# Fused decoder step: first tiles from unnormalised features, and a scan whose decays come from running sums read back from DRAM

## The chip, the cores and the metric

The kernel runs on one core of a Trainium2 chip. The metric is the device time of one execution in microseconds; lower is better. Before the change it is 1802.67 us, the median of three runs (1802.15 to 1803.92). One further execution was recorded by the hardware profiler.

The engines are TensorE (PE, matrix products into PSUM), VectorE (DVE), ScalarE (ACT), GpSimd (POOL) and SyncE (SP). Here SP issues the loads of weights, POOL most other transfers, and ACT a few at the start.

## What is computed

One layer of a hybrid decoder with 2048 features, on 288 tokens: 256 of one prompt and 32 samples (8 branches of 4 tokens, each with its own prior state). Cut to what matters here:

```python
n = rmsnorm(h, g_mix)
proj = n @ w_in                      # z | x, B, C | dt | u | v
xbc = silu(causal_dwconv(xbc, conv0, conv_w, conv_b))
dt = softplus(dt_raw + dt_bias);  A = -exp(a_log)
# scan, chunks of 128 tokens, 4 groups of 8 heads
acum = cumsum(dt * A)
decay = exp(where(tril, acum[l] - acum[s], -inf))
y_diag = einsum(C, B, decay, x * dt)
states = einsum(B, exp(acum[-1] - acum), x * dt)
h_next = h_prev * exp(acum[-1]) + states
y_off  = einsum(C, h_prev, exp(acum))
y = y_diag + y_off + d_skip * x
y_ssd = rmsnorm(y * silu(z))
y_cm = gelu(u) * (tril(W_s) @ rmsnorm(gelu(v)) + b_s)
h = h + concat(y_ssd, y_cm) @ w_out
# then a SwiGLU feed-forward, a gated input embedding and a final norm
```

The outputs are the features of all tokens, the new scan and convolution states, and the sample rows of v.

## The kernel before

Features lie on the 128 partitions, tokens along the free axis. A weight matrix is cut into output tiles of 128 features; each needs 16 blocks of 128x128 weights (more in the feed-forward). float32 accuracy comes from two-part numbers: a tensor is split into `hi` and `lo`, and `mm3` makes three matmuls for each block (L179 hi by hi, L180 activation lo by weight hi, L181 activation hi by weight lo). So a tile of 16 blocks is 48 matmuls of 128x128 by 288. Weights come in halves of 128x1024 (512 KB) by SP's queue into four buffers `raw` (`load`); `split_w` makes `whi` on ACT (L172) and `wlo` on DVE (L173), three buffers of each. Tiles accumulate in three PSUM banks `acc`; the small products share five banks, `big`.

The order of instructions on each engine is set by a scheduler that runs a model of the program; the text of the kernel gives the dependencies and a priority (the splits of weights are put ahead). What each engine then does is a fixed list.

**The start.** Eight slices `xin` of the input are loaded, squared on ACT (L239) and summed over the features by 48 float32 matmuls with one output column each (`sum_tokens`, L102). A chain of small DVE operations makes the norm factor, two steps on PE spread it over the partitions (L118, L120), and DVE multiplies xin by it (L249). Then each slice is split (L150 on ACT, L151 on DVE) and the matmuls of tiles 0, 1 and 2 run slice by slice, with the projection to dt among them (`pdt`, L257). `dt_work` is the softplus, `decay_work` and `decay_sample` (L313) the decays that don't depend on x.

**The scan.** There are four groups of six tiles: B, C and four of x. `conv_tile` copies a tile from PSUM into `cbuf`, applies the convolution (L338 on DVE) and the silu. Then `ssd_group`, cut by `yield` into steps that are run between weight tiles, works on a chunk: ACT writes rows R, a masked triangle times dt·A (L366); PE multiplies them by a triangle (`seg`, L371 and L372), and Exp gives the decays M. PE also transposes x (L384), forms C·B, the chunk's product M·xdt (L398), the state S, C·S of the prior state (L473), which is scaled on DVE and added by an identity matmul (L401). Samples take a segment matmul of their own (L481) and eight new states a group, each one matmul over 128 rows (`new_states`, L417).

**After the scan** come the gate, the v tiles, 16 output tiles whose result is added to h (L707), and the spatial mix. Its weights `wsr` and biases `bsr` (1 MB each) are loaded when the scan's memory is given back (`mlp_pools`, `spatial_weights`), and `wsr` is multiplied by a triangle (L576).

Of the kernel before, what the change touches and what calls it, by code (L numbers as in the profile page):

```python
# [40 lines left out]
def hybrid_step(ctx: ExitStack, tc: tile.TileContext, xT, wa, wd, wple, pT, vec, cst, wdt, dtal,  # L41
# [161 lines left out]
    rmask = csts[:, C_RM:C_RM + 8]  # L203
    TsR, UsR = csts[0:32, C_TS:C_TS + P], csts[0:32, C_US:C_US + P]
    Ts, Us = TsR[:, 0:32], UsR[:, 0:32]
# [31 lines left out]
    for q in range(8):
        sq = s0.tile([P, 2, NT], F32, tag="sq", name="sq", bufs=4)
        nc.scalar.activation(sq, xin[q], AF.Square)  # L239
        for j in range(2):  # L240
            sum_tokens(pss, sq[:, j], first=q + j == 0, last=q + j == 8)
    halves = {at: split_w(raw, 8) for at, raw in first.items()}
    nc.vector.tensor_mul(gw, wdts, bc_in(vecs[:, V_MIX:V_MIX + 16], 32))
# [4 lines left out]
    for q in range(8):
        nc.vector.tensor_mul(xin[q], xin[q], bc_mid(rs0, 2))  # L249
# [17 lines left out]
    Etm = small([P, 2, 32], "Etm")
    dec1 = small([P, 32], "dec1")
    decS = small([P, 8, 32], "decS")
    def dt_work():  # L270
        df = s0.tile([P, 384], F32, name="dtf")
        nc.scalar.copy(df[:, 0:NT], pdt[:, 0:NT])
        nc.vector.tensor_copy(r3(df[:, NT:384], 32), bc_mid(df[:, 256:288], 3))
        pd = big("pd")
# [20 lines left out]
        nc.vector.tensor_copy(dtAh, dtA)  # L295
        nc.vector.tensor_sub(dtAl, dtA, f32(dtAh))
        nc.scalar.copy(Ur, U)

    def decay_work():
        ps = big("pdec")  # L300
        nc.tensor.matmul(ps[:, 0:64], lhsT=U, rhs=dtA[:, 0:2], start=True, stop=True)
        nc.tensor.matmul(ps[:, 64:96], lhsT=UsR, rhs=dtA[0:32, 2], start=True, stop=True)
        nc.tensor.matmul(ps[:, 96:128], lhsT=T1, rhs=dtA[:, 1], start=True, stop=True)
        nc.tensor.matmul(ps[:, 128:160], lhsT=TsR, rhs=dtA[0:32, 2], start=True, stop=True)
        nc.tensor.matmul(ps[:, 160:192], lhsT=ones, rhs=dtA[:, 1], start=True, stop=True)
        nc.scalar.activation(dec.rearrange("p a b -> p (a b)"), ps[:, 0:96], AF.Exp)
        nc.scalar.activation(Etm.rearrange("p a b -> p (a b)"), ps[:, 96:160], AF.Exp)
        nc.scalar.activation(dec1, ps[:, 160:192], AF.Exp)

    def decay_sample():  # L310
        ps = big("pdec")
        for b in range(8):
            nc.tensor.matmul(ps[:, 192 + 32 * b:224 + 32 * b], lhsT=rmask[0:32, b:b + 1].to_broadcast([32, P]),  # L313
                             rhs=dtA[0:32, 2], start=True, stop=True)
        nc.scalar.activation(decS.rearrange("p a b -> p (a b)"), ps[:, 192:448], AF.Exp)
# [611 lines left out]
```

## Time and profile before

| | before |
|---|---|
| median of three runs | 1802.67 us |
| profiled execution | 1801.47 us |
| its span (first to last instruction) | 1799.3 us |
| mean granted clock of TensorE | 0.983 |
| moved by DMA | 297.63 MB, mean 165 GB/s |
| time of ACT on L172, DVE on L173 (weights) | 533.7 us, 623.3 us |

In a row of the trace the left name after the operation is the output and those behind the arrow the inputs; then come the shape and the count. Square brackets give idle time before, and what ended it. A group's row gives busy time and mean nanoseconds. Matmuls overlap, so the distance between two starts says more than a duration. The clock is a share of full speed.

### The profile page before, as it was taken

To read this page: it belongs to the slowest core of one execution; us is meant where nothing else is said; L and a number is where in the kernel's file an instruction comes from. 1 tells how busy PE (TensorE), PEld (TensorE's weight loads), DVE (VectorE), ACT (ScalarE), POOL (GpSimd) and SP (SyncE) were. 2 spreads that over 40 slices of the span, in tenths; PEclk is the share of its full clock that TensorE was granted. 3 is DMA by queue.
4 is the path that set the end of the run, shared out by engine and by line. 5 is a ranking of instruction groups with operands and counts; after the bars stand their busy time and mean duration, and the time that the engine had idled before them with its cause. 6 is when DMAs were issued, how large, how long until landed. Compare 5 with 4: busy or idle time off the path is not lost.

```text
span 1799.3 us, 31672 instructions
## 1 busy us (share of the span) xinstructions
PE 1765.1 (98%) x13084; PEld 1731.5 (96%) x13084; DVE 1062.1 (59%) x1655; ACT 826.9 (46%) x1432; POOL 31.2 (2%) x79
## 2 busy tenths in 40 slices
PE   8999999998999999999999999999999999999996
PEld 7989988978999999999999999999999999999996
DVE  3768687776445686555555554444555555554665
ACT  3585758463345544444333333333333333444452
POOL 0001010101000000000000000000000000000000
PEclk6999999999999999999999999999999999999998
DMA  4536464627555544554555545555555455555452
GB/s 161 180 132 230 133 216 143 223 88 267 165 164 165 165 135 162 165 165 158 167 164 166 165 165 159 166 163 171 167 164 168 163 168 167 161 167 169 164 166 89
DMA packets 83600, 297.63 MB, mean 165 GB/s; under 512 B 9488, under 2 KB 9616, under 8 KB 83200
## 3 DMA queue, kind: packets, MB, share of 16 engines
q1 hardware_dynamic: 75600, 268.85, 46.3%
q0 software_dynamic: 6128, 23.34, 3.6%
q10 hardware_dynamic: 1728, 3.43, 0.5%
q8 instruction: 102, 1.67, 0.4%
q14 instruction: 42, 0.34, 0.1%
HBM read 283.19 MB, written 12.39 MB: 164 GB/s over the span
## 4 chain that ended last, share of the span: by engine, by line
PE 75%; DVE 0%; ACT 0%; DVEq 0%; issue 0%
PE acc L179 25%; PE acc L181 24%; PE acc L180 24%; PE pb L597 0%; PE pb L181 0%; PE pb L179 0%; PE pb L180 0%; PE pb L589 0%; DVE h L829 0%; PE pb L102 0%; PE pb L118 0%; DVE wlo L173 0%; DVE h L707 0%; PE pb L120 0%; DVEq L916 0%
## 5 line engine op out<-in xcount | busy, mean ns | idle before, releaser
L179 PE MATMUL acc<-hi,whi 128*128 128x288 f32 x4000 | 1187.5, 297 | 7.7 <-DVE h L707 4.4
L180 PE MATMUL acc<-lo,whi 128*128 128x288 f32 x4000 | 1184.9, 296 | 0.0
L181 PE MATMUL acc<-hi,wlo 128*128 128x288 f32 x4000 | 1181.0, 295 | 1.2 <-DVE wlo L173 1.2
L172 ACT CAST whi<-raw 128x1024 fp32r<-128x1024 f32 (+1 forms) x516 | 533.7, 1035 | 827.8 <-PE acc L180 664.8
L173 DVE TENSOR_TENSOR wlo<-raw,whi 128x1024 fp32r<-128x1024 f32 (+1 forms) x516 | 623.3, 1208 | 486.2 <-ACT whi L172 479.5
L179 PEld LDWEIGHTS acc<-hi,whi 128*128 128x128 f32 x4000 | 753.1, 188 | 11.7 <-issue 7.3
L181 PEld LDWEIGHTS acc<-hi,wlo 128*128 128x128 f32 x4000 | 755.0, 189 | 3.7 <-DVE wlo L173 1.8
L180 PEld LDWEIGHTS acc<-lo,whi 128*128 128x128 f32 x4000 | 753.8, 188 | 1.5 <-issue 0.6
L783 DVE SCALAR_TENSOR_TENSOR Up<-acc,rs 128x288 f32<-128x288 f32 x44 | 20.1, 457 | 41.9 <-PE acc L181 41.9
L778 DVE TENSOR_TENSOR G<-acc,rs 128x288 f32<-128x288 f32 x44 | 20.1, 457 | 41.6 <-PE acc L181 41.6
L338 DVE SCALAR_TENSOR_TENSOR cva<-cbuf,cwh,cva 128x312 f32<-128x312 f32 x72 | 38.5, 538 | 1.3 <-ACT cva L336 0.4
L551 ACT ACTIVATE gt<-gt 128x288 f32<-128x288 f32 x32 | 14.2, 443 | 40.5 <-DVE gt L550 40.5
L389 ACT ACTIVATE xw<-xdt,dec 128x64 f32<-128x64 f32 x96 | 24.4, 338 | 5.9 <-DVE xdt L386 5.9
L102 PEld LDWEIGHTS pss<-ones,sq 128*128 128x128 f32 x96 | 20.6, 333 | 3.9 <-ACT sq L239 3.9
L102 PE MATMUL pss<-ones,sq 128*128 128x1 f32 x96 | 20.6, 352 | 3.7 <-ACT sq L239 3.7
L418 DVE TENSOR_TENSOR h<-h,pb 128x512 f32<-128x512 f32 x32 | 20.9, 680 | 1.1 <-PE pb L417 1.1
L366 ACT ACTIVATE Rh<-cst,dtAh 128x128 fp32r<-128x128 f32 x64 | 20.6, 397 | 1.5 <-PE pb L371 1.5
L784 DVE TENSOR_TENSOR Up<-Up,G 128x288 f32<-128x288 f32 x44 | 20.2, 458 | 1.5
L366 ACT ACTIVATE Rl<-cst,dtAl 128x128 fp32r<-128x128 f32 x64 | 20.8, 399 | 0.0
L424 DVE TENSOR_TENSOR h<-h,decS 128x512 f32<-128x512 f32 x32 | 20.1, 683 | 0.0
L780 DVE SCALAR_TENSOR_TENSOR G<-Gt,G 128x288 f32<-128x288 f32 x44 | 19.9, 453 | 0.1
L779 ACT ACTIVATE Gt<-G 128x288 f32<-128x288 f32 x44 | 19.4, 441 | 1.2 <-DVE G L778 1.2
(270 smaller groups left out, 927.0 us busy)
## 6 DMA issues: line engine op xcount, KB each, us to landing
raw<-in_wa_dram SPq DMA_DIRECT2D x416, 512.0 KB, 3.6
raw<-in_wd_dram SPq DMA_DIRECT2D x64, 512.0 KB, 3.5
raw<-in_wd_dram SPq DMA_DIRECT2D x32, 384.0 KB, 3.1
h<-in_h0T_dram POOLq DMA_DIRECT2D x16, 512.0 KB, 6.6
out_dram<-h POOLq DMA_DIRECT2D x16, 512.0 KB, 5.9
h<-in_xT_dram POOLq DMA_DIRECT2D x4, 576.0 KB, 7.1
raw<-in_wple_dram SPq DMA_DIRECT2D x4, 512.0 KB, 3.6
xin<-in_xT_dram ACTq DMA_DIRECT2D x4, 288.0 KB, 6.0
```

Of the source, the lines that this page charges most:

```text
L102: nc.tensor.matmul(ps[:, c:c + 1], lhsT=acc[:, t:t + P], rhs=ones[:, 0:1], start=first and c == 0, stop=last and c == 2)
L172: nc.scalar.copy(a, r)
L173: nc.vector.tensor_sub(b, r, f32(a))
L179: nc.tensor.matmul(ps, lhsT=wh, rhs=hi, start=first, stop=False)
L180: nc.tensor.matmul(ps, lhsT=wh, rhs=lo, start=False, stop=False)
L181: nc.tensor.matmul(ps, lhsT=wl, rhs=hi, start=False, stop=last)
L338: nc.vector.scalar_tensor_tensor(ao, cb[:, j:j + NCO], wt[j], ao, op0=ALU.mult, op1=ALU.add)
L366: nc.scalar.activation(cols(r, i), T1, AF.Identity, scale=f32(d[:, c, k + i:k + i + 1]))
L389: nc.scalar.activation(xw[:, 64 * h:64 * h + 64], xd[:, 64 * h:64 * h + 64], AF.Identity, scale=dec[:, c, 8 * g + h:8 * g + h + 1])
L418: nc.vector.tensor_add(h0[q][:, i], h0[q][:, i], ps)
L424: nc.vector.tensor_mul(r3(hh, 64), r3(hh, 64), bc_in(decS[:, 2 * q + i, hs], 64))
L784: nc.vector.tensor_mul(u, u, G)
```

## The change

**Start.** Tiles 0 to 5 take splits of xin times gain without the norm factor (`x_act`); the factor is multiplied in afterwards, where a tile is copied out of PSUM (now on DVE) and in `dt_work`. The loads of xin and of quarter weights alternate on SP's queue, vec and the first four xin go by ACT's, and wdt, cst, dtal and scv by POOL's. Squares are added up on DVE and summed by one set of matmuls over tokens. The normalised splits `n_act` for the later tiles are made after that.

```diff
+def first_w(m, j):
+    nc.sync.dma_start(raws[m, j // 2][:, 512 * (j % 2):512 * (j % 2) + 512],
+                      wa[m, :, 4 * j:4 * j + 4].rearrange("p k m -> p (k m)"))
+nc.scalar.dma_start(vecs, vec)
 for q in range(8):
-    (nc.scalar if q % 2 else nc.sync).dma_start(xin[q], xT[:, 2 * q:2 * q + 2])
+    (nc.scalar if q < 4 else nc.sync).dma_start(xin[q], xT[:, 2 * q:2 * q + 2])
+    if q % 2 == 0:
+        for m in range(3):
+            first_w(m, q // 2)
-        for j in range(2):
-            sum_tokens(pss, sq[:, j], first=q + j == 0, last=q + j == 8)
+            x_act.append(split(xk, gain=vcol(V_MIX, k)))
+            for m in range(3):
+                if k % 4 == 0:
+                    quarter(m, k // 4)
+                mm3(ps01[m], halves[m, k // 8], k % 8, x_act[k], k == 0, k == KD - 1)
...
+    nc.scalar.activation(sq, xin[q], AF.Square)
+    if q:
+        nc.vector.tensor_add(sqa, sqa, sq)
+nc.vector.tensor_add(sqa[:, 0], sqa[:, 0], sqa[:, 1])
+rs0 = bcast_tokens(rstd_compact(sqa[:, 0], 2048.0, EPS, "rm"))
 for q in range(8):
     nc.vector.tensor_mul(xin[q], xin[q], bc_mid(rs0, 2))
     for k in (2 * q, 2 * q + 1):
+        n_act.append(split(xin[q][:, k % 2], gain=vcol(V_MIX, k), tags=LONG))
...
-    nc.scalar.copy(df[:, 0:NT], pdt[:, 0:NT])
+    nc.vector.tensor_mul(df[:, 0:NT], pdt[:, 0:NT], rs0)
...
-    nc.scalar.copy(cb[:, 3:259], ps[:, 0:256])
+    if rs is None:
+        nc.scalar.copy(cb[:, 3:259], ps[:, 0:256])
+    else:
+        nc.vector.tensor_mul(cb[:, 3:259], ps[:, 0:256], rs[:, 0:256])
...
-    ps = ps01[at] if at < 3 else mtile(wa[at], n_act)
+    ps = ps01[at] if at < 3 else mtile(wa[at], n_act if g else x_act)
```

**Scan.** The running sums of dt·A are made once by PE, written to DRAM (`cdram`) and read back for each group onto all 128 partitions (`cq`, 8 heads by 288 tokens, 1.18 MB, on SP's queue). A decay is then Exp of −Relu(cum − cq), on ACT, and needs no x, so it is written ahead of the group's other steps. The prior state enters `y_chunk(1)` as products of S with C·exp(cum). The sample rows are packed so that a branch pair has 32 rows, and the eight new states are matmuls over 32 rows, four side by side. The small decays are one matmul set less.

```diff
-def make_R(c, hb):
...
-        nc.scalar.activation(cols(r, i), T1, AF.Identity, scale=f32(d[:, c, k + i:k + i + 1]))
-    nc.tensor.matmul(ps, lhsT=Ur, rhs=R[0], start=True, stop=False)
-    nc.tensor.matmul(ps, lhsT=Ur, rhs=R[1], start=False, stop=True)
-    nc.scalar.activation(M, ps, AF.Exp)
+            nc.scalar.activation(cols(M, i), cq[:, h, c * P:(c + 1) * P], AF.Relu, scale=-1.0,
+                                 bias=cum[:, c, 8 * g + h:8 * g + h + 1])
+        nc.scalar.activation(M, M, AF.Exp, scale=-1.0)
...
+nc.scalar.copy(crow, pc[0:32, 0:NT])
+nc.gpsimd.dma_start(cdram, crow)
...
+nc.sync.dma_start(cq, cdram[hs].unsqueeze(0).to_broadcast([P, 8, NT]))
...
-nc.tensor.matmul(ps, lhsT=cols(Cf, 1), rhs=S, start=True, stop=True)
-yoE = scaled(ps, 0)
+nc.scalar.activation(CE, CE, AF.Exp)
+nc.vector.tensor_mul(CE, CE, bc_mid(cols(Cf, 1), 8))
+nc.vector.tensor_sub(Msm, Msm, bc_in(cum[:, 2, hs], 32))
...
-            nc.tensor.matmul(cols(py, j), lhsT=cols(yoE, j), rhs=ident, start=False, stop=True)
+                l, r = (xd, cols(M[h // 4], h % 4)) if w == 0 else (off[0], off[1][:, h])
...
-nc.tensor.matmul(ps[0:32, 0:256], lhsT=Us, rhs=Rs.rearrange("p a b -> p (a b)"), start=True, stop=True)
...
-    nc.tensor.matmul(ps, lhsT=bm, rhs=xst, start=True, stop=True)
+    for q in range(4):
+        r = slice(32 * q, 32 * q + 32)
+        nc.tensor.matmul(pss[q], lhsT=bm[r], rhs=xst[r], start=True, stop=True, tile_position=(32 * q, 0))
```

**Elsewhere.** The pool of the convolution's buffers is its own, opened at the start. The product of wsr with the triangle stands in `spatial` and no longer in `spatial_weights`:

```diff
 def spatial_weights(mp):
-    nc.vector.tensor_mul(w, w, bc_mid(T1, KD))
 def spatial(nv, mp, bss, wss, w, b):
+    nc.vector.tensor_mul(w, w, bc_mid(T1, KD))
```

**The order on the engines.** First PE at the start of the program (`ps` and `acc` are the banks of the first three tiles, `pss` the sums of squares, `pb` the spread factor, `pdt` the dt projection). Before:

```order
L224 MATMUL warm<-ones 128x128 x14
L102 MATMUL pss<-ones,sq 128x1 x48
L118 MATMUL pb<-cst,rmy 128x128 x2
L120 MATMUL pb<-cst,rmy 128x32
L179 MATMUL ps_224<-hi,whi 128x288
L179 MATMUL ps_225<-hi,whi 128x288
L179 MATMUL acc<-hi,whi 128x288
L257 MATMUL pdt<-xin_82,gw 32x288 x2
```

And now, where L186 to L188 are the three lines of `mm3`, and L284 is the dt projection:

```order
L236 MATMUL warm<-ones 128x128 x14
L186 MATMUL ps_142<-hi,whi 128x288
L187 MATMUL ps_142<-lo,whi 128x288
L186 MATMUL ps_143<-hi,whi 128x288
L187 MATMUL ps_143<-lo,whi 128x288
L284 MATMUL pdt<-xin_85,gw 32x288 x2
L188 MATMUL ps_142<-hi,wlo 128x288
L188 MATMUL ps_143<-hi,wlo 128x288
```

The weight matmuls stand right behind the warm-up, with nothing for the norm ahead of them.

Next DVE, from the normalised activations on: before, the last activation lo's and then dt_work between the weight lo's.

```order
L151 SCALAR_TENSOR_TENSOR lo<-xin_89,vec,hi 128x288 x2
L273 COPY dtf<-dtf 128x96
L173 TENSOR_TENSOR wlo<-raw,whi 128x1024
L279 TENSOR_TENSOR dtwx<-pd,dtal 128x32 x3
L173 TENSOR_TENSOR wlo<-raw,whi 128x1024
L280 SCALAR_TENSOR_TENSOR dtwt<-dtwx 128x96
L173 TENSOR_TENSOR wlo<-raw,whi 128x1024
```

Now, from the second last pair of activation lo's; in front of this stand the eight products of xin (L296), the dt product (L314), three conv buffers (L382 and L383, one pair a tile) and the first twelve lo's with one weight lo:

```order
L158 SCALAR_TENSOR_TENSOR lo<-xin_91,vec,hi 128x288 x2
L158 SCALAR_TENSOR_TENSOR lo<-xin_92,vec,hi 128x288 x2
L180 TENSOR_TENSOR wlo<-raw,whi 128x1024 x2
L389 SCALAR_TENSOR_TENSOR cva<-cbuf,cwh,cva 128x312 x2
L322 TENSOR_TENSOR dtwx<-pd,dtal 128x32 x3
L389 SCALAR_TENSOR_TENSOR cva<-cbuf,cwh,cva 128x312 x2
L323 SCALAR_TENSOR_TENSOR dtwt<-dtwx 128x96
L180 TENSOR_TENSOR wlo<-raw,whi 128x1024
L389 SCALAR_TENSOR_TENSOR cva<-cbuf,cwh,cva 128x312 x2
L333 TENSOR_SCALAR dtwx<-dtwx 128x96
L325 TENSOR_SCALAR dtww<-dtwt 128x96
L382 TENSOR_TENSOR cbuf<-acc,rs 128x256
```

The convolution (`cva`) and the copies out of the banks now stand between the weight lo's, and the bank of the fourth tile is read only at the last row.

Last DVE at the first output tiles (`cvo` are the gated features, `rs` their norm factor). Before:

```order
L173 TENSOR_TENSOR wlo<-raw,whi 128x1024
L542 TENSOR_TENSOR cvo<-cvo,rs 128x288 x4
L151 SCALAR_TENSOR_TENSOR lo<-cvo,vec,hi 128x288 x4
L576 TENSOR_TENSOR wsr<-wsr,cst 128x2048
L707 TENSOR_TENSOR h<-h,acc 128x288 x3
L173 TENSOR_TENSOR wlo<-raw,whi 128x1024 x4
```

And now:

```order
L180 TENSOR_TENSOR wlo<-raw,whi 128x1024
L593 TENSOR_TENSOR cvo<-cvo,rs 128x288 x4
L158 SCALAR_TENSOR_TENSOR lo<-cvo,vec,hi 128x288 x4
L759 TENSOR_TENSOR h<-h,acc 128x288 x3
L633 TENSOR_TENSOR wsr<-wsr,cst 128x2048
L180 TENSOR_TENSOR wlo<-raw,whi 128x1024 x4
```

The product of wsr has gone from ahead of three additions to h to behind them; the weight lo's stand behind it in both.

More of the change, by code (lines that the diff above doesn't have):

```diff
@@ L202, in hybrid_step @@
     I4 = csts[:, C_I4:C_I4 + 32]
[L203 to L205 removed]
+    rmask, first8 = csts[:, C_RB:C_RB + 2], csts[:, C_R0:C_R0 + 8]
+    sgB, loB, sgX, loX = (csts[:, C_SG + i:C_SG + i + 1] for i in range(4))
+    TP, UP, TE = (csts[:, c:c + P] for c in (C_TP, C_UP, C_TE))
+    Ts = TE[:, 0:32]
     bmask = csts[:, C_BM:C_BM + 256]
@@ L294, in dt_work @@
         nc.vector.scalar_tensor_tensor(dtA, dt, -1.0, bc_mid(ea, 3), op0=ALU.mult, op1=ALU.mult)
-        nc.vector.tensor_copy(dtAh, dtA)
-        nc.vector.tensor_sub(dtAl, dtA, f32(dtAh))
-        nc.scalar.copy(Ur, U)
     def decay_work():
+        pc = big("pcum")
+        for c in range(2):
+            nc.tensor.matmul(pc[0:32, c * P:(c + 1) * P], lhsT=dtA[:, c], rhs=T1, start=True, stop=True)
+        nc.tensor.matmul(pc[0:32, 256:288], lhsT=dtA[:, 2], rhs=Ts, start=True, stop=True)
+        nc.scalar.copy(crow, pc[0:32, 0:NT])
@@ L300, in decay_work @@
+        nc.gpsimd.dma_start(cdram, crow)
         ps = big("pdec")
         nc.tensor.matmul(ps[:, 0:64], lhsT=U, rhs=dtA[:, 0:2], start=True, stop=True)
[L302 to L305, printed above, removed]
+        nc.tensor.matmul(ps[:, 64:96], lhsT=UP, rhs=dtA[:, 2], start=True, stop=True)
@@ L306, in decay_work @@
+        nc.tensor.matmul(ps[:, 96:160], lhsT=T1, rhs=dtA[:, 0:2], start=True, stop=True)
+        nc.tensor.matmul(ps[:, 160:192], lhsT=TP, rhs=dtA[:, 2], start=True, stop=True)
+        nc.tensor.matmul(ps[:, 192:224], lhsT=TE, rhs=dtA[:, 2], start=True, stop=True)
+        nc.tensor.matmul(ps[:, 224:256], lhsT=ones, rhs=dtA[:, 1], start=True, stop=True)
         nc.scalar.activation(dec.rearrange("p a b -> p (a b)"), ps[:, 0:96], AF.Exp)
-        nc.scalar.activation(Etm.rearrange("p a b -> p (a b)"), ps[:, 96:160], AF.Exp)
@@ L308, in decay_work @@
-        nc.scalar.activation(dec1, ps[:, 160:192], AF.Exp)
+        nc.scalar.copy(cum.rearrange("p a b -> p (a b)"), ps[:, 96:192])
+        nc.scalar.activation(EtmS, ps[:, 192:224], AF.Exp)
+        nc.scalar.activation(dec1, ps[:, 224:256], AF.Exp)
     def decay_sample():
+        nc.vector.tensor_mul(decS, bc_mid(dtA[:, 2], 8), bc_in(first8, 32))
         ps = big("pdec")
-        for b in range(8):
-            nc.tensor.matmul(ps[:, 192 + 32 * b:224 + 32 * b], lhsT=rmask[0:32, b:b + 1].to_broadcast([32, P]),
-                             rhs=dtA[0:32, 2], start=True, stop=True)
@@ L315, in decay_sample @@
-        nc.scalar.activation(decS.rearrange("p a b -> p (a b)"), ps[:, 192:448], AF.Exp)
+        nc.tensor.matmul(ps[:, 0:256], lhsT=ones, rhs=decS.rearrange("p a b -> p (a b)"), start=True, stop=True)
+        nc.scalar.activation(decS.rearrange("p a b -> p (a b)"), ps[:, 0:256], AF.Exp)
     sd_box = {}
@@ L323, in samples, with conv_tile @@
         return ap[:, 259:NCV].rearrange("p (b t) -> p b t", t=7)[:, :, 0:4]
-    def conv_tile(i, ps):
-        sd = sd_box["pool"]
-        cb, a, t = (sd.tile([P, NCV], F32, tag=n, name=n, bufs=b) for n, b in (("cbuf", 3), ("cva", 2), ("cvt", 2)))
+    def conv_tile(i, ps, rs=None):
+        cb, a, t = (cvp.tile([P, NCV], F32, tag=n, name=n, bufs=b) for n, b in (("cbuf", 3), ("cva", 2), ("cvt", 2)))
         nc.gpsimd.memset(cb[:, 0:3], 0.0)
@@ L432, in ssd_group @@
         brep = rep4(sd, Bf[:, 256:288])
-        R0 = [make_R(0, hb) for hb in range(2)]
+        M0 = decay(0)
         yield
@@ L514, in ssd_group @@
         for q in range(4):
-            new_states(q)
-            if q % 2:
-                yield
+            decay_h0(q)
+        yield
+        for i in range(2):
+            new_states(i)
+            yield
     ycat = [None] * 32
@@ L680, in hybrid_step @@
             at += 1
-            conv_tile(i, ps)
+            conv_tile(i, ps, None if g else rs0)
             advance(1)
```

214 lines of the change are left out of this document (118 added, 96 removed).

## The prediction

> **What bounds the kernel now.** I read the page's busy shares first, then a window over a stretch of the middle, then windows over each place where TensorE (PE) is not dense.
>
> ```profile
> PE 1765.1 (98%) x13084; PEld 1731.5 (96%) x13084; DVE 1062.1 (59%) x1655; ACT 826.9 (46%) x1432; POOL 31.2 (2%) x79
> ```
>
> ```profile
> 1000.00:1400.00 400.00, 400.00 (x3010) 400.00 (x3009) 204.55 (x248) 148.16 (x171) 0.00 (x0) 1.00 0.52 165
> ```
>
> PE is busy nearly always. The second row's columns are length, then busy time and count of PE, PE's loads, DVE (VectorE), ACT, POOL, then clock, DMA share and GB/s. In the middle, 3010 matmuls take 400 us: 0.133 us each, at full clock, with DVE half idle. The 12,000 matmuls of the weight tiles (three for each 128x128 block) are untouched by the change; at that pace they need 1595 us. What can be won is everything else: the start, stalls, and PE's small matmuls.
>
> ```profile
> 8.00:10.00 2.00, 0.00 (x0) 0.00 (x0) 0.00 (x0) 0.00 (x0) 0.00 (x0) 1.00 1.06 399
> 10.00:36.00 26.00, 22.13 (x102) 21.91 (x102) 7.04 (x18) 8.25 (x13) 0.00 (x0) 0.51 0.47 164
> 36.00:38.00 2.00, 1.12 (x7) 0.84 (x11) 2.00 (x4) 1.71 (x4) 0.00 (x0) 0.50 0.00 0
> 42.00:44.00 2.00, 2.00 (x18) 2.00 (x17) 2.00 (x6) 1.50 (x4) 0.00 (x0) 1.00 0.00 0
> 365.00:375.00 10.00, 5.54 (x27) 4.90 (x26) 5.20 (x11) 9.97 (x33) 0.00 (x0) 0.69 0.30 104
> 430.00:440.00 10.00, 5.12 (x22) 4.56 (x21) 6.79 (x7) 2.79 (x3) 0.00 (x0) 0.68 0.47 168
> 0.00:86.00 86.00, 28.78 (x96) 18.67 (x96) 0.80 0.49 170
> ```
>
> The last row counts the third matmul of each block (L181) alone: 96, six tiles of sixteen blocks, end by 86.0 us. At the pace of the middle six tiles take 38 us.
>
> ```profile
> 10.91 20.64 PE L102 MATMUL pss<-ones,sq 128*128 128x1 f32 x96 [3.69 <-ACT sq L239]
> 36.88 0.85 PE L179 MATMUL ps<-hi,whi 128*128 128x288 f32 x2 [1.42 <-ACT hi L150]
> ...
> 368.06 0.50 PE L372 MATMUL pb<-Rl,Ur 128*128 128x512 f32 x1 [1.60 <-ACT Rl L366]
> ...
> 432.09 2.29 DVE L576 TENSOR_TENSOR wsr<-wsr,cst 128x2048 f32<-128x2048 f32 x1 [5.00 <-DMA wsr<-in_wsT_dram]
> 434.30 1.18 DVE L707 TENSOR_TENSOR h<-h,acc 128x288 f32<-128x288 f32 x3
> ```
>
> So PE spends 20.64 us on sums of squares, the first weight matmul starts at 36.88, and two stalls lie further on: one for ACT's rows R (L366), one where DVE waits for the DMA of wsr.
>
> **Part A, the start.** The first six tiles no longer need the norm factor, so PE can begin when xin, vec and the first quarter weights are there.
>
> ```profile
> L150 ACT ACTIVATE hi<-xin,vec 128x288 fp32r<-128x288 f32 x16 | 6.9, 521 | 14.2 <-DVE xin L249 14.2
> L239 ACT ACTIVATE sq<-xin 128x576 f32<-128x576 f32 x8 | 5.1, 677 | 11.2 <-DMA cst<-in_cst_dram 7.5 <-PE pss L102 1.9 <-ACT Ur L297 1.0
> L497 ACT CAST xst<-xw 128x512 fp32r<-128x512 f32 x4 | 2.5, 615 | 0.1
> L151 DVE SCALAR_TENSOR_TENSOR lo<-xin,vec,hi 128x288 fp32r<-128x288 f32 x16 | 7.0, 512 | 0.0
> L249 DVE TENSOR_TENSOR xin<-xin,pb 128x576 f32<-128x576 f32 x8 | 5.4, 750 | 1.6 <-PE pb L120 1.6
> L173 DVE TENSOR_TENSOR wlo<-raw,whi 128x1024 fp32r<-128x1024 f32 x484 | 592.6, 1225 | 476.0 <-ACT whi L172 469.4 <-PE pb L120 3.9
> L338 DVE SCALAR_TENSOR_TENSOR cva<-cbuf,cwh,cva 128x312 f32<-128x312 f32 x72 | 38.5, 538 | 1.3 <-ACT cva L336 0.4
> L591 DVE TENSOR_TENSOR vt<-pb,rvy 128x256 f32<-128x256 f32 x16 | 6.6, 417 | 0.4 <-PE pb L589 0.4
> ```
>
> (The group rows give total busy time and count, so 6.9/16 = 0.43 us for a hi, 5.1/8 = 0.64 for a square, 7.0/16 = 0.44 for a lo, 5.4/8 = 0.68 for an xin product.) The first loads move at 399 GB/s at 8 to 10 us, so I put the first matmul at 9. Then three engines run side by side. ACT: 16 hi 6.9, 12 quarter casts at 0.615 (L497, the same shape) 7.4, 8 squares 5.1, together 19.4, and 1.5 of small copies: about 21 from 7, ending at 28. DMA: some 6.8 MB at 399 GB/s, 17 us and the latency, 19 to 22. PE: 146 matmuls by 0.133 = 19.4, the dt projection 2.7 (16 fp32 matmuls packed four side by side; an estimate, not under the 2.1 of 16 at the pace of the middle), and 2.3 of half clock, since the clock is 0.50 at 36 us and 1.00 at 42, some five microseconds after the first matmul. PE is at the sum over tokens at 9 + 24.4 ≈ 33.5. The order puts the broadcast of the factor 48 matmuls later (6.4, and 0.8 for the chain on DVE beyond them): rs0 is out at about 40.7.
>
> Only then can DVE empty the accumulators, and it has much to do first. By the order the pieces are: 8 xin products 5.4; dt product 0.5 and 3 conv buffers at 0.6, both after L591's 0.417 for 256 columns out of PSUM, 2.3; 16 lo for the normalised features 7.0; 4 weight lo's 4.9; 6 cva 3.2; a copy and small dt operations 0.6; the fourth conv buffer 0.6. That is 24.0 us: the last buffer is written at 64.7, its bank comes free, and tile 7 starts. Tile 4 stands ahead of the broadcast, so from 40.7 PE has only tiles 5 and 6, 12.8 us, until 53.5. It waits 11 us in all: some 6 at tile 5, whose weight lo stands behind the eleventh activation lo, the rest before tile 7. Restarting at half clock costs 1 to 2, so 66.5 against 86.0: −19.5. The decays, in the 86 us before, now come behind that point:
>
> ```profile
> 69.94 1.97 PE L313 MATMUL pdec<-dtA,cst 32*128 32x32 f32 x16
> ```
>
> Eight took 1.97 (two records each), 0.25 apiece. Now nine such and one over 256 columns: taken as ten of 0.24, +2.4. **A = −17.1.** Between −29 (DVE never late, 12 us less) and 0 (half clock throughout).
>
> The sentences of this paragraph carry no number of the sum. The Trainium skill, "TensorE: Matmul & The Clock Gate", Part 1, says that the clock starts at half rate and is released after about 3.4 us of sustained activity. The 36 to 44 us rows agree roughly; the 10 to 36 us row does not, with PE recorded busy for 22.13 of 26 us at clock 0.51 (its matmuls have one column). By the page the cold start would cost 1.7 us, by the row that continues up to 17; the second rival below is the row's case.
>
> **Part B, PE's matmuls in the scan, four groups.** Start-to-start times, at full clock:
>
> ```profile
> 117.45 0.39 PE L371 MATMUL pb<-Rh,Ur 128*128 128x512 f32 x1
> 117.68 0.60 PE L384 MATMUL pb<-cst,cvo 128*128 128x128 f32 x4
> ...
> 126.70 1.02 PE L473 MATMUL pb<-S,cvo 128*128 128x512 f32 x2
> 127.56 1.02 PE L477 MATMUL pb<-xw,btm 128*128 128x512 f32 x2
> 128.51 0.62 PE L481 MATMUL pb<-Rs,cst 32*32 32x256 f32 x2
> 129.06 0.66 PE L384 MATMUL pb<-cst,rep 128*128 128x128 f32 x4
> ...
> 131.76 0.44 PE L398 MATMUL pb<-M,xdt 128*64 128x128 f32 x4
> 132.13 0.49 PE L401 MATMUL pb<-cst,yoE 128*128 128x128 f32 x2
> 132.55 0.44 PE L398 MATMUL pb<-M,xdt 128*64 128x128 f32 x4
> ...
> 145.51 0.62 PE L417 MATMUL pb<-xst,bm 128*128 128x512 f32 x2
> 145.97 0.30 PE L181 MATMUL acc<-hi,wlo 128*128 128x288 f32 x1
> ```
>
> Removed: eight segment matmuls a group at 0.23 (L371 to L384), 1.84; C·S, 0.86 (L473 to L477); the sample segment, 0.55 (L481 to L384). Replaced: in y_chunk(1) four identity matmuls of 0.42 (L401 to L398) by four more pairs at 0.37 (L398 to L401), −0.2. The new states stay eight matmuls of 512 columns, before 0.23 each (two in 0.46); now each contracts over 32 rows, four side by side. Nothing before shows four such tiles: between no gain (0) and the time of two of eight (−1.4 a group). The nearest row, L417, stands at no gain, so I take −0.5 a group. Together −4 × (1.84 + 0.86 + 0.55 + 0.2 + 0.5) ≈ **−15.8** (−12 to −19).
>
> Beside it, and outside the sum: the Trainium skill, "TensorEngine Tiling (Array Packing)", Key Properties, says tiles work in parallel but that a change of tiling mode drains the array. The L477 row, 0.95 up to a 32x32 matmul, against L473's 0.86 would be 0.09 a change; at some sixteen changes in a group that is 5.8 over four groups if each drains, while full parallelism would give the −5.6 of the other bound.
>
> **Part C, the stalls.** Around 368 PE idled 4.46 us in the ten shown and ran some 17 matmuls at 0.24 instead of 0.133, 1.8 more. R is gone, and decays now need only dt, so they can run before the conv tiles end: −6.5. Of the wsr stall (4.88 idle, about 2 of half clock) the change moves the product in the code, but the order shows it at the same tile on DVE, only behind the three h additions instead of before them. PE waits there for an accumulator freed by L707, so it gets on while DVE waits for wsr, until the weight lo behind the product is missed: about 2.3 + 1.2 us earlier at best, or nothing. I take −2 (0 to −7, if wsr lands in time because the scan ends otherwise). **C = −8.5** (−4 to −13).
>
> **Part D, new costs.** The decays become ACT work of the same count (8 Relu of 128x128 and 2 Exp in place of 16 R operations and 2 Exp a chunk), the mask products stay, and DVE gets two products of 128x1024 more (1.2 each) a group; both lie beside PE's 6.4 us a tile. What hides them is three weight buffers ahead, each of 24 matmuls by 0.133, 9.6 us; a run of DVE work longer than that shows. I take **+2** (0 to +14).
>
> Sum: −17.1 − 15.8 − 8.5 + 2 = −39.4. The profiled execution took 1801.47 (its span 1799.3), so 1762.1; the median of the runs lies 1.2 above that execution, which gives **1763**.
>
> **The rivals.**
> - *DVE is hidden at the start* (17%): the scheduler's buffers let weight lo's pass, the waits of 11 us and a microsecond of restart vanish: 1763 − 12 = 1751. For it: ACT and DVE were both half idle (10 to 36 us row). Against: the order has the lo's in front.
> - *The clock stays at half in the new start* (8%): 146 matmuls cost 0.133 more, +19, of which some is absorbed in DVE's chain: A ≈ 0, 1780. For it the 0.51 row; against it the dense matmuls that reached 1.00 in five microseconds.
> - *A new wait in each scan group* (12%): after y_chunk(1) DVE has about 22 operations (11 us) with no weight lo between; beyond the 9.6 us PE waits about 2 and restarts at half clock, 3 in all, in each of four groups: 1763 + 12 = 1775. This rests on the wsr row, where 8.5 us of DVE delay cost 4.4 of idle PE.
> - *Slower than before: the read-back queue* (3%). Each group's cumulative sums go to all partitions by one 1.18 MB transfer on SP's queue, ahead of raw weights. Its own share at 399 GB/s is 3 us. The nearest row is a broadcast that took 14.7:
>
> ```profile
> bsr<-in_bsP_dram POOLq DMA_DIRECT2D x1, 1024.0 KB, 14.7
> ```
>
>   That one had loads ahead of it. If a read-back held the queue for L us, PE would lose 4 × (L − 9.6) and half-clock restarts; from L about 18.5 on, with 1 us each, the 39 us gained are gone, so 1803 and more.
>
> That the change doesn't remove what it says is excluded, as the order no longer has L366 to L372 nor the 48 matmuls of L102.
>
> **How the numbers follow.** Forecast 60%, its own range 1753 to 1772. The range takes in the hidden chain and the new wait, 1746 to 1780, and leaves out most of the clock and queue cases with the tails. A measurement of this kernel can tell about 0.2%, 3.6 us, from no change. The cases below 1799: 0.95; within: 0.02; slower: 0.03.
>
> **What would show it.** Right: first weight matmul near 9, tile 7 near 66, DVE named as releaser before tiles 5 and 7; no idle like that around 368; PE's small matmuls shorter by 16 in sum. Wrong: clock at 0.5 beyond 20 us; weight lo's or raw DMAs ending PE's idle time in the scan; the stall at wsr as long as before.

## The result, and the profile after

The changed kernel takes **1755.88 us** (median of four runs, 1753.28 to 1756.97) against 1802.41 of the kernel before in the same comparison: a ratio of 0.9739, 95% interval 0.9722 to 0.9756. The forecast was 1763 in a range of 1746 to 1780. The profiled execution took 1753.28 us with a span of 1751.5, so it lies 2.6 us below the median; set against the profiled execution of before (1801.47) it gains 48.2 where the sum said 39.4.

To find where the time went I cut both spans at the same work: at the start of the 7th, the 43rd and the 49th weight tile, counted by the third matmul of each block.

| stretch | before | after | difference |
|---|---|---|---|
| start to the 7th tile | 86.2 | 66.6 | −19.6 |
| 7th to 43rd (the scan) | 312.5 | 288.6 | −23.9 |
| 43rd to 49th (wsr, last gate) | 52.2 | 48.3 | −3.9 |
| the rest | 1348.4 | 1348.0 | −0.4 |

The page of the changed kernel, busy time and the clock in 40 slices:

```profile
PE 1721.6 (98%) x12972; PEld 1693.2 (97%) x12972; DVE 1070.9 (61%) x1693; ACT 812.4 (46%) x1363; POOL 33.9 (2%) x84
...
PEclk9999999999999999999999999999999999999998
```

The busy shares say nothing: 98% before and after. What changed shows in windows (length; busy time and count of PE, its loads, DVE, ACT, POOL; clock, DMA share, GB/s):

```profile
10.00:36.00 26.00, 26.00 (x173) 20.41 (x169) 21.53 (x37) 18.84 (x39) 0.00 (x0) 0.94 0.83 291
66.61:355.18 288.57, 286.68 (x2266) 268.69 (x2265) 242.82 (x483) 196.09 (x501) 17.98 (x49) 1.00 0.60 202
355.18:403.47 48.29, 43.71 (x307) 40.68 (x306) 31.53 (x57) 19.24 (x32) 6.34 (x12) 1.00 0.75 267
```

In the first row PE is recorded busy for all of 26 us, yet it has only 173 records, where the pace of the middle would give 195: part of it runs at half clock and part waits for loads and splits between matmuls, and the record stretches over both. The start itself, on PE and then on DVE:

```profile
8.55 0.40 PE L186 MATMUL ps<-hi,whi 128*128 128x288 f32 x1 [1.54 <-ACT whi L267]
...
35.62 0.72 PE L109 MATMUL pb<-ones,sqa 128*128 128x1 f32 x6
42.41 0.61 PE L125 MATMUL pb<-cst,rmy 128*128 128x128 f32 x4
...
54.77 0.64 PE L318 MATMUL pd<-cst,dtf 128*128 128x32 f32 x2 [3.41 <-DVE dtf L315]
56.77 0.61 PE L188 MATMUL acc<-hi,wlo 128*128 128x288 f32 x1 [1.35 <-DVE wlo L180]
...
66.27 0.37 PE L186 MATMUL acc<-hi,whi 128*128 128x288 f32 x1 [1.17 <-DVE cbuf L383]
```

```profile
43.63 5.44 DVE L296 TENSOR_TENSOR xin<-xin,rs 128x576 f32<-128x576 f32 x8 [1.22 <-ACT rs L132]
...
55.49 1.22 DVE L180 TENSOR_TENSOR wlo<-raw,whi 128x1024 fp32r<-128x1024 f32 x1
...
65.60 0.42 DVE L382 TENSOR_TENSOR cbuf<-acc,rs 128x256 f32<-128x256 f32 x1
```

The first weight matmul is at 8.55 instead of 36.88. The sum over tokens is issued at 35.62, the factor is spread at 42.41, and from 43.63 on DVE works through its list; three waits on PE (3.41, 1.35, 1.17), each ended by DVE, stand before the seventh tile.

In the scan, the rows of the second chunk's y products and of the new states:

```profile
338.59 0.44 PE L448 MATMUL pb<-cq,S 128*64 128x128 f32 x4
338.86 0.39 PE L448 MATMUL pb<-M,xdt 128*64 128x128 f32 x4
339.08 0.39 PE L448 MATMUL pb<-cq,S 128*64 128x128 f32 x4
339.30 0.39 PE L448 MATMUL pb<-M,xdt 128*64 128x128 f32 x4
```

```profile
135.37 0.49 PE L465 MATMUL pb<-M,bm 32*128 32x512 f32 x1
135.79 0.40 PE L186 MATMUL acc<-hi,whi 128*128 128x288 f32 x1
...
299.42 0.29 PE L187 MATMUL acc<-lo,whi 128*128 128x288 f32 x1
299.65 0.50 PE L465 MATMUL pb<-M,bm 32*128 32x512 f32 x4
300.08 0.41 PE L186 MATMUL acc<-hi,whi 128*128 128x288 f32 x1
300.32 0.30 PE L187 MATMUL acc<-lo,whi 128*128 128x288 f32 x1
```

A pair of y products (four records, two a matmul) now stands 0.22 us from the next one, not 0.37; all have one shape (128 rows by 64 columns). Each pair of `cq` and S adds to the PSUM columns that the pair before it has just written, and that costs no time that shows. One state tile of 32 rows takes 0.42 us and four side by side take 0.43, so they do run in parallel; but the weight matmul ahead of them lasts 0.23 us to the next start instead of 0.13, and the one behind them 0.24.

What PE waited for, in us in total, times and the longest, between 66.5 and 360 us:

```profile
PE acc L186 <- DVE cbuf L383: 1.2, 1, 1.2
PE acc L186 <- ACT whi L179: 1.0, 2, 0.5
PE pb L448 <- DVE M L425: 0.7, 1, 0.7
PE pb L525 <- ACT xw L436: 0.2, 1, 0.2
```

and between 360 and 404:

```profile
PE acc L188 <- DVE wlo L180: 2.3, 3, 1.2
PE acc L186 <- ACT whi L179: 2.3, 3, 1.4
```

The wait for the rows R is gone, and none of the scan's waits reaches 1.3 us (the 1.2 is the one ahead of the seventh tile). The last stretch still loses 4.6 us, now named after weight splits and not after the wsr transfer.

### The profile page after: what moved, and what is told of

It reads as the page before. It is cut to its first block, busy times and chain, and to the rows that moved or that the text cites. A ratio compares the mean times of both kernels' runs of the same rounds, so it can differ in the third digit from the quotient of the medians.

```text
span 1751.5 us, 31442 instructions
## 1 busy us (share of the span) xinstructions
PE 1721.6 (98%) x12972; PEld 1693.2 (97%) x12972; DVE 1070.9 (61%) x1693; ACT 812.4 (46%) x1363; POOL 33.9 (2%) x84
## 4 chain that ended last, share of the span: by engine, by line
PE 77%; DVE 0%; ACT 0%; DVEq 0%; issue 0%
PE acc L186 25%; PE acc L188 25%; PE acc L187 25%; PE pb L648 0%; PE pb L188 0%; PE pb L186 0%; PE pb L187 0%; PE pb L640 0%; PE pb L109 0%; DVE h L881 0%; PE pb L125 0%; PE pb L127 0%; DVEq L978 0%; DVE rot L88 0%; DVE roy L90 0%
## 5 line engine op out<-in xcount | busy, mean ns | idle before, releaser
L186 PE MATMUL acc<-hi,whi 128*128 128x288 f32 x4000 | 1187.2, 297 | 4.5 <-ACT whi L179 3.2
L188 PE MATMUL acc<-hi,wlo 128*128 128x288 f32 x4000 | 1177.5, 295 | 3.7 <-DVE wlo L180 3.7
L179 ACT CAST whi<-raw 128x1024 fp32r<-128x1024 f32 (+1 forms) x510 | 528.2, 1036 | 825.4 <-PE acc L187 665.1
L180 DVE TENSOR_TENSOR wlo<-raw,whi 128x1024 fp32r<-128x1024 f32 (+1 forms) x510 | 615.6, 1208 | 477.8 <-ACT whi L179 467.1
L186 PEld LDWEIGHTS acc<-hi,whi 128*128 128x128 f32 x4000 | 751.1, 188 | 11.9 <-ACT whi L179 5.8
L188 PEld LDWEIGHTS acc<-hi,wlo 128*128 128x128 f32 x4000 | 753.3, 188 | 7.0 <-DVE wlo L180 4.5
L602 ACT ACTIVATE gt<-gt 128x288 f32<-128x288 f32 x32 | 14.2, 443 | 40.7 <-DVE gt L601 40.7
L436 ACT ACTIVATE xw<-xdt,dec 128x64 f32<-128x64 f32 x96 | 24.1, 338 | 6.8 <-DVE xdt L433 6.8
L418 ACT ACTIVATE M<-cq,cum 128x128 f32<-128x128 f32 x64 | 19.9, 390 | 8.4 <-DMA cq<-cdram 8.3
L164 DVE TENSOR_TENSOR lo<-Up,hi 128x288 fp32r<-128x288 f32 x44 | 19.9, 451 | 0.0
L163 ACT CAST hi<-Up 128x288 fp32r<-128x288 f32 x44 | 19.1, 434 | 1.4 <-DVE Up L836 0.5
L840 DVE TENSOR_TENSOR h<-h,acc 128x288 f32<-128x288 f32 x32 | 14.5, 454 | 6.4 <-PE acc L188 6.4
```

What stands on the lines that cost most here:

```text
L179: nc.scalar.copy(a, r)
L180: nc.vector.tensor_sub(b, r, f32(a))
L186: nc.tensor.matmul(ps, lhsT=wh, rhs=hi, start=first, stop=False)
L188: nc.tensor.matmul(ps, lhsT=wl, rhs=hi, start=False, stop=last)
L436: nc.scalar.activation(xw[:, 64 * h:64 * h + 64], xd[:, 64 * h:64 * h + 64], AF.Identity, scale=dec[:, c, 8 * g + h:8 * g + h + 1])
```

## The experiments

The runs of before that stand beside each batch had medians of 1802.44, 1802.79 and 1802.20 us.

**The two halves apart.** First the new start on the old scan:

```diff
 # the kernel before, with the diff's section "Start" alone
+ps = ps01[at] if at < 3 else mtile(wa[at], n_act if g else x_act)
+conv_tile(i, ps, None if g else rs0)
```

> The kernel before with the new start alone (unnormalised first six tiles, squares summed on ACT and DVE, loads interleaved); the scan is the old one. Theory (the two halves of the change act apart): the seventh tile starts near 66.6 us instead of 86.2, the segment matmuls and the stall near 366 us (some 20 us earlier) stay, the old decays come behind the seventh tile (+2 to +3): about 1785 us, 1782 to 1788. Rival (the new start only looks good because the lighter scan lets DVE catch up behind it): the old scan's work piles up, and most of the 20 us are given back in the first scan group: above 1793 us.

1786.32 us (ratio 0.9906, 0.9891 to 0.9921). The seventh tile starts at 67.9; from there to the 49th 370.0 us against 364.7 of before, of which the old decays, now behind the seventh tile, take 3.5. The theory's number, and no pile-up. Then the new scan on the old start:

```diff
 # the changed kernel, with the start of before
-ps = ps01[at] if at < 3 else mtile(wa[at], n_act if g else x_act)
-conv_tile(i, ps, None if g else rs0)
+ps = ps01[at] if at < 3 else mtile(wa[at], n_act)
+conv_tile(i, ps)
```

> The changed kernel with the old start (normalised first tiles, 48 square sums on PE); the scan and the wsr product are the new ones. Theory: the first tiles as before, seventh tile near 86 us, then the scan 28 us shorter from there on, less the 2.4 us of decays that lie ahead of the seventh tile again: about 1772 us, 1769 to 1776; PE's small matmuls between the seventh and the 49th tile sum to some 52 us against 82. Rival (what the scan gains is only the stall of 366 us and a smaller wsr stall, and the shorter matmuls are eaten by new waits): about 1792 us.

1767.08 us (0.9801, 0.9784 to 0.9817), 2 below the expected band. The small matmuls between the 7th and the 49th tile sum to 49.1 us against 82.1 before. The scan is the larger half: −35.4 of its own, the start −16.1. Together they would be −51.5, and the joint change has −46.5. That these 5 us are lost where the two meet is not shown, since each of the three numbers has an interval of about 3 us to either side. If they are, the traces say where: from the 7th to the 43rd tile the joint kernel takes 288.6 us and this one 281.7, and only 2.4 of the difference are the decays.

**The shape of neighbours.** The changed kernel with the old way of adding the prior state:

```diff
-py1 = y_chunk(1, xd1, M1, (S, CE))
+nc.tensor.matmul(ps, lhsT=cols(Cf, 1), rhs=S, start=True, stop=True)
+py1 = y_chunk(1, xd1, M1, yoE)     # an identity matmul behind each pair
```

> The changed kernel with the prior state of the prompt added in the old way: C times S (one matmul of 512 columns), a product on DVE by the decay, and an identity matmul behind each pair of y matmuls; the product of C with exp(cum) is left out. Theory (a change of the shape of matmuls costs as much as the matmul): pairs and identities go back to 0.37 and 0.42 us, that is (0.79 - 0.44) x 16 = +5.6 us, C times S +2.6 to +3.4 us, together 8 to 9 us on PE and about 1764 us. Rival (the removed matmul C times S and four identities at 0.21 are all there is to it, the shape costs nothing): 2.6 + 16 x (0.21 - 0.22), under 3 us, about 1758 us.

1759.95 us (1757.87 to 1762.03), +4.1: between the two. In its trace y products and identities take 16.4 us instead of 12.1, C times S 3.75, and the stretch from the start to the 49th tile is 6.5 longer; the part behind is 1.9 shorter. So the price on PE is nearer to the theory, and the median doesn't settle it. The next run does, with the order changed in the kernel before (the start and stop flags follow the order):

```diff
-                                     rhs=cols(M[h // 4], h % 4), start=True, stop=yoE is None)
-                if yoE is not None:
-                    nc.tensor.matmul(cols(py, j), lhsT=cols(yoE, j), rhs=ident, start=False, stop=True)
+                                     rhs=cols(M[h // 4], h % 4), start=yoE is None or j == 0, stop=yoE is None)
+            if yoE is not None:
+                for j in range(4):
+                    nc.tensor.matmul(cols(py, j), lhsT=cols(yoE, j), rhs=ident, start=False, stop=j == 3)
```

> The kernel before with one change of order: in the second chunk the four identity matmuls stand behind the four pairs of y matmuls, not one behind each pair. The same matmuls are made. Theory (shape changes cost): four pairs at 0.22 and four identities at 0.21 and two changes at 0.15 to 0.2 make about 2.1 us in place of 3.16 a group, over four groups -4.2 us, about 1798 us. Rival (the identity matmul itself is dear): no change, 1802.4 us.

1798.32 us (0.9977, 0.9967 to 0.9986; ten runs), and on PE's timeline:

```profile
128.11 1.09 PE L398 MATMUL pb<-M,xdt 128*64 128x128 f32 x16
129.37 1.05 PE L402 MATMUL pb<-cst,yoE 128*128 128x128 f32 x8
130.35 1.92 PE L494 MATMUL pb<-h,Cb 128*32 128x512 f32 x16
```

Four pairs in 1.26 us and four identities in 0.98, together 2.24 where the alternating order took 3.16. Over all groups pairs and identities fall from 17.91 to 13.75 us: −4.2 on PE, −4.1 in the median. The same matmuls in another order: the change of shape is what was paid. Another reading, that an identity has to wait for the pair whose columns it adds to, doesn't fit the changed kernel, where pairs add to columns just written and still start 0.22 us apart.

**The row tiles.** New states over 128 rows, as before, in the changed kernel (`bmk` holds eight masks, one a state, in columns added to cst):

```diff
-for q in range(4):
-    nc.tensor.matmul(pss[q], lhsT=bm[r], rhs=xst[r], start=True, stop=True, tile_position=(32 * q, 0))
+    nc.scalar.activation(bm, f32(bst), AF.Identity, scale=bmk[:, 2 * q + i:2 * q + i + 1])
+    nc.tensor.matmul(pss[q], lhsT=bm, rhs=xst, start=True, stop=True)
```

> The changed kernel with each new state as one matmul over all 128 rows against a masked B (eight masks a group instead of two), in place of four tiles of 32 rows side by side. Theory (in the changed kernel's trace four tiles side by side take 0.43 us together and a single one 0.42, a 128-row matmul took 0.23 before): 32 x 0.233 = 7.5 us on PE against 6.6, so +1 us, about 1757 us: the row tiles gain little since eight of 32 stand alone. Rival (they are what carried the scan's gain): +5 us or more, 1761 us.

**1745.81 us** (two runs, 1745.15 and 1746.47), 10 below the changed kernel: neither theory. On PE the 32 matmuls take 7.5 us and the weight matmuls beside them keep their 0.13; but the stretch from the 7th to the 43rd tile hardly changes (287.9 against 288.6), and the gain is from the 43rd to the 49th tile, with 40.5 us instead of 48.3. In this kernel's order four weight lo's stand on DVE between the splits of the last gate and the wsr product, in the changed kernel none. That suggested the next run:

```diff
-nc.vector.tensor_mul(w, w, bc_mid(T1, KD))
...
+if m == 8:
+    nc.vector.tensor_scalar(one, h[:, m, 0:1], 0.0, 1.0, op0=ALU.mult, op1=ALU.add)
+    nc.vector.scalar_tensor_tensor(sw[2], sw[2], one, bc_mid(T1, KD), op0=ALU.mult, op1=ALU.mult)
```

> The changed kernel with the product of wsr and the triangle made to depend on the ninth addition to h (a column of ones made from it), some 50 us later. Theory (the wait near 387 us, in which weight lo's stand behind this product, costs about 7 us, and the previous run with 128-row states was fast only because the product stood one tile later there): from the 43rd to the 49th tile 41 us instead of 48.3, 1749 us. Rival (the 128-row states were faster by themselves): no change, 1754 to 1757 us.

1750.99 us (1750.44 to 1753.13), 4.9 below the changed kernel and near the theory's 1749. But its stretch takes 46.3 us and not 41: in these two executions the wsr product is 2 of the 7.8 us between 48.3 and 40.5, and the rest has another cause. With both edits:

> The late wsr product and the 128-row states together. Theory: the states alone now, +1 us on the kernel with the late product alone (7.5 against 6.6 us on PE), about 1750 us. Rival (the row tiles cost more than their own time, by the masks or by PSUM banks held): 1745 us or less, below the kernel with the late product by 4 or more.

**1745.88 us** (0.9684, 0.9670 to 0.9698), 5.1 below the late product alone: the rival held, and the wsr product makes no difference beside the 128-row states (with these states alone DVE waits 3.3 us for wsr, and PE not at all). The stretch is 40.5 again, all of it busy, as its window shows:

```profile
355.30:395.80 40.50, 40.50 (x306) 40.32 (x305) 27.58 (x52) 20.37 (x35) 6.33 (x12) 1.00 0.87 317
```

What differs there is when the last gate's norm factor is spread (L125): at 377.85 in the changed kernel and at 372.57 here. The windows up to that moment, for the third matmul of each block alone (PE and its loads, clock, DMA share, GB/s), of the changed kernel:

```profile
0.00:377.85 377.85, 212.00 (x720) 136.03 (x720) 0.99 0.61 207
```

and of the run with both edits:

```profile
0.00:372.57 372.57, 209.80 (x712) 134.69 (x712) 0.99 0.60 205
```

720 is 45 tiles to the last block, 712 half a tile less. The lo splits of the last gate's features (L158 on DVE, behind the products L593) start 3.8 us behind the factor in the changed kernel and 2.7 here; of the open tiles the changed kernel has no block left to run over them. With the late product alone the factor comes at 720 blocks too. That this half tile is the whole of the 5 us is read from the traces; no run changed it alone.

**The read-back.**

```diff
 nc.sync.dma_start(cq, cdram[hs].unsqueeze(0).to_broadcast([P, 8, NT]))
+nc.sync.dma_start(cq, cdram[hs].unsqueeze(0).to_broadcast([P, 8, NT]))
```

> The changed kernel with each group's read-back of the running sums issued twice in a row on SP's queue (the second overwrites the first with the same values). Theory (weights are loaded far enough ahead): four times 1.18 MB more, some 3 us of the queue each, behind 9.6 us of weights that are ready: no change, 1754 to 1758 us. Rival (the read-back already starves the weight loads): each doubled load costs PE its 3 us and a restart, 4 x 3 to 4 x 5, 1768 us or more, with DMA raw as releaser.

1759.15 us (1754.28 to 1760.39), one microsecond above the theory's band and 3.3 above the changed kernel. The two intervals overlap (0.9739 to 0.9770 and 0.9722 to 0.9756), so a cost of some 3 us for the second read is neither shown nor excluded; the rival's 12 us and more are not there. A read-back lands in 7.3 us in the changed kernel, and here:

```profile
cq<-cdram SPq DMA_DIRECT2D x8, 1152.0 KB, 6.6
```

**The clock.**

```diff
-for _ in range(14):
+for _ in range(1):
     nc.tensor.matmul(wu[:, 0:P], lhsT=ones, rhs=ones, start=True, stop=True)
```

> The changed kernel with one warm-up matmul in place of 14. Theory (in its first eight microseconds PE waits for loads, and the clock rises within some five microseconds of dense matmuls): the clock is at half until about 14 us, three tiles end less than 2 us later and the chain of the norm follows: 1756 to 1758 us. Rival (only the warm-up brings the clock up; without it PE stays at half through the first tiles, as before): the sum over tokens comes 10 us or more later, 1766 us or more.

1754.37 us (1752.78 to 1756.86), below the theory's band and within the changed kernel's own spread: the warm-up is worth nothing that shows here. And 30 of them in the kernel before:

> The kernel before with 30 warm-up matmuls in place of 14, so that PE is busy up to the first square sums at about 10.9 us instead of idle from 7. Theory (the one-column matmuls of the square sums don't keep the clock up, whatever comes ahead of them): clock about 0.5 between 14 and 36 us again, 1801 to 1804 us. Rival (the idle stretch from 7 to 10.9 us dropped the clock): clock near 1.0 from 10 us on, the square sums and the first tiles shorter, some 5 us or more faster, 1797 us or less.

1799.82 us (0.9984, 0.9974 to 0.9993), 1 below the band. PE's idle time ahead of the square sums is 0.3 us instead of 3.7, and the clock falls under them all the same:

```profile
10.00:12.00 2.00, 1.72 (x16) 1.53 (x14) 0.22 (x1) 2.00 (x4) 0.00 (x0) 1.00 1.04 404
12.00:14.00 2.00, 2.00 (x16) 2.00 (x15) 0.52 (x1) 2.00 (x4) 0.00 (x0) 0.75 1.00 339
14.00:16.00 2.00, 2.00 (x11) 2.00 (x11) 1.32 (x2) 0.69 (x2) 0.00 (x0) 0.50 1.05 416
```

The warm-up matmuls, 0.11 us apart, run at full clock up to 10.1 us; the square sums begin at 10.68, 0.11 us apart too and with the same 128x128 weights, but with one column for 128, and from 12.9 on they stand 0.21 apart. So the old start ran at half clock because of its one-column matmuls; the idle time ahead of them was worth the 3.0 us gained here at the most.

**DVE's list at the start.**

```diff
+with tc.high_priority(offset=300):
     rs0 = bcast_tokens(rstd_compact(sqa[:, 0], 2048.0, EPS, "rm"))
+with tc.high_priority(offset=-400):
     # products of xin and splits of n_act
```

> The changed kernel with another priority: the norm factor's chain first, the normalised splits last, so that DVE reads the first three banks out before the eight xin products, and the fifth tile's weight lo stands ahead of the normalised lo's. Theory (DVE's list after the factor is what holds the seventh tile, with waits of 3.4, 1.4 and 1.2 us and half clock after them): the wait of 3.4 goes, the seventh tile starts near 62 us instead of 66.6, 1751 us. Rival (the DVE work is only moved, the fourth bank is read out no earlier): seventh tile at 65 to 67, 1754 to 1757 us.

1755.87 us (1753.95 to 1757.98), the changed kernel's own time: the rival. What PE waited for from 36 to 130 us:

```profile
PE acc L186 <- ACT cvo L395: 8.1, 1, 8.1
PE pb L450 <- DVE M L427: 1.4, 1, 1.4
PE acc L188 <- DVE wlo L180: 1.3, 2, 0.7
```

The three waits became one of 0.6 and one of 8.1, the latter before the seventh tile, which now starts near 67.6; the fourth bank is read out at 66.34 by DVE, against 65.60. The releaser's name (a small copy on ACT) is what came last by the record; the bank's own readout on DVE ended beside it. DVE's some 23 us of work behind the factor, without a gap, are the chain in both orders. Neither order has the fourth bank's readout ahead of the splits, so what that would gain stays open. Last, this priority with the late wsr product:

> Both of these: norm chain first and the late wsr product. Theory: the two act 300 us apart and add up, 4 + 7 us, about 1745 us. Rival (either is given back behind it): 1749 us or more.

1752.56 us (0.9723, 0.9708 to 0.9737), 3.3 below this priority alone: the rival, with no more than the late product's gain. The best version of all is the changed kernel with 128-row states, at 1745.8 to 1745.9 with or without the late product.

## Why the prediction was right, and where it was not

**A, the start: the mechanism right; right to 0.1 us by luck, since its steps err against each other.** 66.5 was forecast for the seventh tile and 66.6 came; in the other runs with the new start it lies between 65.2 and 68.0. The first matmul was put at 9 and came at 8.55. The sum over tokens came 2 us late (35.6 against 33.5) and the factor 2.9 late, at 43.6 on DVE against 40.7. DVE's list then took 22.5 us up to the end of the fourth readout, against 24.0. The 1.8 of half clock, which the sum added behind that list, fell into the wait instead (weight matmuls 0.24 us apart from 57 to 61 us) and cost nothing at its end. PE's waits were 6.0 instead of 11. The run with another priority shows the step that carries it: shuffling the list moved the waits and not the seventh tile. Half clock was no threat to the first matmuls: the dense start reached full clock by 14 us, with one warm-up matmul as with 14.

**B, PE's matmuls in the scan: right mechanism, wrong size.** This is the term that was mis-sized: −15.8 forecast, −24.1 measured (7th to 49th tile; start-to-start times by line; the segment matmuls are put at 0.23 each, and what L371 and L372 took above that stands under C).

| part | forecast | measured |
|---|---|---|
| segment matmuls | −7.4 | −7.4 |
| C·S | −3.4 | −2.6 |
| sample segment | −2.2 | −2.2 |
| y products and identities | −0.8 | −5.8 |
| new states | −2.0 | −0.9 |
| others (sample y −2.3, S −1.5, transposes −1.0, C·B −0.5) | 0 | −5.2 |

The step that failed says that four more pairs cost "0.37" each. I took the start-to-start time of a pair out of the old rows, where an identity of another shape follows every pair; without it all pairs, the old ones too, fall to 0.22. The experiment with the identities last shows this alone: −4.2. The sample products are the same case (L506 and L508 alternated before). The new states were put at a gain of 2.0 and gave 0.9 in their own lines; the weight matmuls next to them lengthen by 2.7 us in all, so with their neighbours the row tiles cost 9.3 us against 7.7 before, a loss of 1.6 on PE; with 128-row states in the changed kernel it is 7.5 again. The Trainium skill, "TensorEngine Tiling (Array Packing)", Key Properties, says both, that tiles work in parallel and that a change of mode drains the array; the rows 0.42 and 0.43 agree with the first, 0.23 against 0.13 with the second. The prediction's paragraph on it had the price right (0.09 a change) and did not let it into the sum.

**C, the stalls: the size right, the causes in part.** L371 and L372 took 6.1 us above their 0.23 each. Of this 4.9 lie in the stall near 368, with 1.8 of half clock behind it: 6.7 against the 6.5 taken. The other 1.2 are starts 0.34 to 0.43 us apart, beside small matmuls, and belong to B. But R ended only the first 1.60 of that stall's idle time; the next row of before shows what ended the rest:

```profile
371.41 0.61 PE L179 MATMUL acc<-hi,whi 128*128 128x288 f32 x1 [2.86 <-DVE zr L526]
```

`zr` is the gate's product on DVE, which reads the bank that PE needs next. It stands there behind a split that waits for ACT, and on ACT four rows of R (1.2 us) and eight products for the state (1.9 us) stand ahead of that split's other half. So how much of the 2.86 was R's is not shown; in the changed kernel's trace neither wait is left.

In the stretch of the second stall the weight matmuls lost 2.3 less, forecast −2, and in the profiled execution wsr's product starts without a wait:

```profile
387.42 2.28 DVE L633 TENSOR_TENSOR wsr<-wsr,cst 128x2048 f32<-128x2048 f32 x1
```

That need not be so in every execution. Here the transfer of wsr landed 11.0 us after its issue. In the run with the norm first, whose profiled execution took 1757.59 us, it took 13.8; DVE waited 1.2 us for it, and the stretch took 51.9 us, as long as in the kernel before. The changed kernel's other three executions took 1.6 to 3.7 us longer than the profiled one. That they wait for wsr would explain why the late product gains 4.9 us in the median and 2 in the trace, but no trace of them is there to show it. What remained there without that wait is not what I believed: by the traces it is the last gate's norm.

**D, new costs: the size came out by luck, the mechanism did not hold.** Over their pace, the weight matmuls from the 7th to the 43rd tile took 2.3 us more than before, net of the 1.8 of half clock that went, against +2. The step that put this on runs of DVE work longer than the weight buffers is not what the trace shows: no wait in this stretch names a weight lo, and DVE ended one of 0.7 us (M). 2.0 us lie beside the row tiles of this stretch.

The decays behind the seventh tile took 2.4, as forecast. Summed (start, B, decays, the segment's lines, the second stall, D, the rest): −19.6 − 24.1 + 2.4 − 6.1 − 2.3 + 2.3 − 0.4 = −47.8, the difference of the two spans. The forecast's sum was −39.4; of the 8.4 us between the two, 8.3 are B's.

**The rivals.** DVE hidden at the start: no, PE waits for it in both orders. Half clock through the new start: no. A new wait in each group: no, the longest in the scan is 0.7 us, once. The read-back slower than before: no; read twice, its median is 3.3 us higher, which is not clear of the noise and far from the 12 of that test's rival.

## What to carry to other kernels

The time of a small matmul read out of a trace belongs to its neighbours too: before you price one that is removed or added, look whether the ones beside it have the same shape, and group equal shapes. Where one engine works off a list and the step that frees a buffer stands at its end, the sum of the list is the forecast, and another order of the rest moves only the waits. And when a scheduler writes the order, an edit in one place can move a chain elsewhere by half a tile: compare at equal work, stretch by stretch, before an edit is given the credit.

## What the hardware showed that was not expected

A change to 32-row tiles and back costs the weight matmul ahead 0.09 us and the one behind 0.11 (0.22 and 0.24 to the next start, where the middle has 0.133). A 32-row tile over 512 columns takes 0.42 us where a matmul over 128 rows takes 0.23, so four tiles in parallel save half, not three quarters. With one warm-up matmul the clock column reads 1.00 from the first microsecond, while weight matmuls that follow each other stand 0.24 us apart up to 11.9 us and 0.13 from 14.1 us on:

```profile
9.32 0.44 PE L186 MATMUL ps<-hi,whi 128*128 128x288 f32 x1
9.56 0.44 PE L187 MATMUL ps<-lo,whi 128*128 128x288 f32 x1
...
15.08 0.29 PE L187 MATMUL acc<-lo,whi 128*128 128x288 f32 x1
15.21 0.29 PE L188 MATMUL acc<-hi,wlo 128*128 128x288 f32 x1
```

So in a stretch without an earlier change of clock the spacing of matmuls is the better clock. The Trainium skill, "TensorE: Matmul & The Clock Gate", Part 1, has the clock follow PE's activity; the rows with 30 warm-up matmuls add that a PE recorded busy without a gap from 10.7 us on, with one-column matmuls, stands at 0.50 from 13 us on.
